# Norm sums behind the first product, gate transposes in the pool mixer, the last down third by tokens, and operands placed with their weights

## The chip, the cores and the metric

One core of one Trainium2 chip runs the whole program. The metric is the device time of one execution in microseconds (us). TensorE (PE) multiplies; PEld is its weight load, which overlaps; VectorE (DVE), ScalarE (ACT) and GpSimd (POOL) work elementwise; SyncE (SP) only issues DMAs, and so does ACT for some.

## The reference

Two transformer blocks in fp32 on x of 512 tokens by 1024 features, one after the other:

```
first_block:  u = rms_norm(x, norm_in_g);  pool_x, pool_z, m_x, m_z = split(u @ w_in)
              y_pool = pool_mixer(pool_x) * silu(pool_z)
              y_m    = mlstm(m_x: conv, headwise q/k/v, gates, both directions) * silu(m_z)
              h = rms_norm(x + [y_pool, y_m] @ w_out, norm_out_g)
second_block: h += nsa_mixer(rms_norm(h, norm_mix[0]))          # three attention branches
              h += conv_ffn(rms_norm(h, norm_ffn[0]))           # layer 0
              h += swa_mixer(rms_norm(h, norm_mix[1]))          # window 128, sinks
              h += conv_ffn(rms_norm(h, norm_ffn[1]))           # layer 1
              return rms_norm(h, norm_final)
conv_ffn(h):  a, u = split(h @ w_gu);  (silu(causal_conv3(a)) * u) @ w_down     # 2816 wide
rms_norm(x,g) = x * rsqrt(mean(x*x) + 1e-6) * g
```

## The kernel before

Activations lie feature-major: `H` is [128 partitions, 8 chunks of features, 512 tokens]. Every operand of a product is split into a rounded high part (`xh`, `wh`: a cast on ACT) and a rest (`xl`, `wl`: a subtraction on DVE). `linear` makes one 128x512 output from 8 chunks (6 or 8 in the down product) by three matmuls each, `mm3`: wh·xh (L108), wh·xl (L109), wl·xh (L110), so 24 matmuls of 128 rows by 512 columns. The activation moves, the weight is stationary. A unit of weights (`raw`, L93: 512 KB by an SP DMA into `wr`; `wh`, L102; `wl`, L103) feeds one linear; `wr`, `wh` and `wl` have 3 buffers each.

An rms norm is not applied before the product. `norm_x` splits H times its gain, the products run on that, and each result is multiplied by the row `rb` of 1/rms per token when it leaves PSUM. `rb` comes from `norm_r`: eight squares on ACT (`accsq`, L182), seven additions (L187, six on POOL and the last on DVE, 3 buffers `sq`), a column sum on PE (`colsum`, L152), a Newton iteration on DVE (L140 to L146), a broadcast on PE (`bcast`, L159) and a copy on ACT (L162). At each of the five norms two linears are issued ahead of `norm_r`, and their results wait in PSUM (six banks for linears: two `mm`, three `S`, one `po`).

Stages in order: `first_block` (the 8 m_x linears with a conv, `gates`, the pool mixer, mLSTM, w_out), `nsa`, `ffn(0)`, `swa`, `ffn(1)`, the final norm. `gates` makes a chain of scans on DVE of 36 rows (`gi`, `gB`, `gM`) and transposes gi and gB by eight small matmuls (L294, L295); the columns are used in mLSTM.

The feed-forward takes its 22 hidden chunks in segments of 8, 8 and 6: up(0), up(1), down(0), up(2), down(1), then the last third. Before, `down_last` runs it for tokens 0 to 255, then for 256 to 511: 16 linears of 18 matmuls of 256 columns, each with its own unit of 768 columns, loaded and split twice. `final_half` (squares L1192, additions L1194, column sum L1199, Newton, broadcast L1205, copy L1208, scaling L1214 to L1217, DMA L1218) follows for each half of the tokens, the first one in the middle of the second half's linears.

The order on each engine is a scheduler's: it takes the instructions in code order with their dependences and moves them by readiness, so one product's matmuls may stand inside another's. Where a tile lies in a partition of SBUF follows from the order in which the pools `con`, `per`, `wp` and those of the stages hand out tiles, summed up in bytes: before, `xh`, `xl`, `wh` and `wl` begin at multiples of 128 bytes, the `gh` and `gl` of the feed-forward 64 bytes past one, the pool mixer's `yph` and `ypl` 96 past one, and mLSTM's `mqh`, `mql`, `mkh`, `mkl` 32 past one.

Of the kernel before, what the change touches and what calls it, by code (L numbers as in the profile page):

```python
# [11 lines left out]
F32 = mybir.dt.float32  # L12
# [19 lines left out]

class Model:
    def __init__(self, ctx, tc, a, out, stop=None):
# [18 lines left out]
    def first_loads(self):  # L53
        nc, a = self.nc, self.a
        vec = self.con.tile([128, a["vecs"].shape[1]], F32, name="vec")
        nc.scalar.dma_start(vec, a["vecs"])
        nc.sync.dma_start(self.H[:, 0:1, :], a["xT"][:, 0:1, :])
        self.first = self.unit(a["w_in"], 0)
        for k0, k1 in ((1, 2), (2, 4), (4, 6), (6, 8)):
            nc.sync.dma_start(self.H[:, k0:k1, :], a["xT"][:, k0:k1, :])  # L60
        self.vec, self.voff = vec, VOFF

# [85 lines left out]

    def colsum(self, acc):
# [45 lines left out]
    def norm_r(self):  # L195

        acc = None
        for k in range(KC):
            acc = self.accsq(k, acc)
        y = self.rstd(acc)  # L200
# [63 lines left out]
    def gates(self, lp, pp, gps):  # L264
        nc = self.nc
        V, G, S, PE = nc.vector, nc.gpsimd, nc.scalar, nc.tensor
        t = lambda s: pp.tile([36, T], F32, name=s)
        g, lf, ex, B, M = t("gi"), t("lf"), t("gex"), t("gB"), t("gM")
# [21 lines left out]
        V.tensor_copy(identr, self.ident[:36, :36])  # L290
        tp = self.tp_ps([128, 2, NT, 36])
# [8 lines left out]
        self.gate_tiles = (gcol, ecol, nmh, nml, identr)  # L300

    def pool_mixer(self, pp, xh, xl, rb):
        nc, a = self.nc, self.a
        V, G, S, PE = nc.vector, nc.gpsimd, nc.scalar, nc.tensor
        W = T + 16
        pinv = pp.tile([128, 4, 16], F32, name="pinv")
# [4 lines left out]
        for g, w in enumerate(POOL_WINDOWS):  # L311
# [3 lines left out]
            for i in range(2):  # L315
# [20 lines left out]
                pl.append(l)  # L336
            if g % 2 == 0:
                pw = self.unit(a["pool_w"], g // 2)
# [183 lines left out]
    def mid_norm_r(self):  # L522
# [13 lines left out]
        rb = self.per.tile([128, T], F32, name=self.n("rb"), tag="rb", bufs=1)  # L536
        self.bcast(y2, rb)
        return rb, y1

    def rot_half(self, pool, src):  # L540

        r = self.per.tile([128, T], F32, name=self.n("rot"), tag="sq", bufs=3)
# [4 lines left out]
    def rope(self, pool, ps, cs, out, bias=None):  # L547
        V, G, S = self.nc.vector, self.nc.gpsimd, self.nc.scalar
        x = self.per.tile([128, T], F32, name=self.n("sq"), tag="sq", bufs=3)
# [85 lines left out]
    def nsa(self):  # L635
        tc, nc, a = self.tc, self.nc, self.a
        V, G, S, PE = nc.vector, nc.gpsimd, nc.scalar, nc.tensor
        with tc.tile_pool(name="nsa", bufs=1) as ap:
            self.attn_consts(ap)
# [19 lines left out]
            pre = [self.linear(a["nsa_w"], i, xh, xl, wide=True) for i in range(2)]  # L659
            rb, y1 = self.mid_norm_r()  # L660
# [75 lines left out]
            def cproj(kv, pre=None):  # L736
                blk = [ap.tile([128, 8, 124], F32, name=self.n("blk"), tag="p", bufs=4) for _ in range(2)]
                for m in range(2):
                    ps = pre[m] if pre else self.linear(a["nsa_w"], 2 * kv + m, xh, xl, wide=True)
# [27 lines left out]
            bk = cproj(0, pre)  # L767
# [75 lines left out]
    def cmp_vals(self, ap, p, pc, vbd):  # L843
# [6 lines left out]
        pct = self.per.tile([64, T], F32, name=self.n("pct"), tag="sq", bufs=3)  # L850
# [117 lines left out]
    def swa_tables(self):  # L968
        tc, nc, a = self.tc, self.nc, self.a
        V, G = nc.vector, nc.gpsimd  # L970
        ap = self.swa_early = self.ctx.enter_context(tc.tile_pool(name="swae", bufs=1))
# [14 lines left out]
    def swa(self):  # L986
# [4 lines left out]
        with tc.tile_pool(name="swa", bufs=1) as ap:  # L991
            cs = (cos, sin)
            xh, xl = self.norm_x("norm_mix1")
            pre = [self.linear(a["swa_w"], i, xh, xl, wide=True) for i in range(2)]
            rb = self.norm_r()
            Q, O = {}, {}

            def proj(i, wide=False):
                ps = pre[i] if i < 2 else self.linear(a["swa_w"], i, xh, xl, wide=wide)
# [120 lines left out]
            wo(1, range(8), True)  # L1120


    def ffn(self, l):
        tc, nc, a = self.tc, self.nc, self.a
        V, G, S, PE = nc.vector, nc.gpsimd, nc.scalar, nc.tensor
        if l:
            self.fin = self.ctx.enter_context(tc.tile_pool(name="fin", bufs=1))
        with tc.tile_pool(name=f"ffn{l}", bufs=1) as fp:
            xh, xl = self.norm_x(f"norm_ffn{l}")
            pre = [self.linear(a[f"ffn_gu{l}"], i, xh, xl, wide=True) for i in range(2)]  # L1130
            rb = self.norm_r()
            cw, cb = f"ffn_cw{l}", f"ffn_cb{l}"

            def up(seg):
                f0, nf = SEGS[seg]
                gh, gl = [], []
                for f in range(f0, f0 + nf):
                    ps = pre[0] if f == 0 else self.linear(a[f"ffn_gu{l}"], 2 * f, xh, xl, wide=True)
# [9 lines left out]
                    ps = pre[1] if f == 0 else self.linear(a[f"ffn_gu{l}"], 2 * f + 1, xh, xl, wide=True)  # L1148
# [12 lines left out]
            def down_last(g):  # L1161

                nf = SEGS[2][1]
                for hf in range(2):
                    c = slice(256 * hf, 256 * hf + 256)
                    gh, gl = [[x[:, c] for x in g[i]] for i in range(2)]
                    for m in range(KC):
                        ps = self.linear(a[f"ffn_d{l}2"], m, gh, gl, nk=nf, wide=True, n=256)
                        V.tensor_tensor(self.H[:, m, c], ps[:, :256], self.H[:, m, c], op=OP.add)
                        if hf and m == 3:  # L1170
                            self.final_half(0)
# [5 lines left out]
            down(1, g1)  # L1177
            if l:
                down_last(g2)
            else:  # L1180
                down(2, g2)

    def final_half(self, hf):

        nc, fp = self.nc, self.fin
        V, G, S, PE = nc.vector, nc.gpsimd, nc.scalar, nc.tensor
        W, nb = 256, 2
        c = slice(W * hf, W * hf + W)
        acc = None
        for k in range(KC):  # L1190
            d = fp.tile([128, W], F32, name=self.n("fs"), tag="fs", bufs=3)
            S.activation(d, self.H[:, k, c], AF.Square)  # L1192
            if k:
                V.tensor_tensor(acc, acc, d, op=OP.add)  # L1194
            else:
                acc = d
        ps = self.tp_ps([128, nb])
        for j in range(nb):
            PE.matmul(ps[:, j:j + 1], acc[:, j * 128:(j + 1) * 128], self.ones, start=True, stop=True)  # L1199
        var = self.con.tile([128, nb], F32, name=self.n("fv"), tag="fv", bufs=2)  # L1200
        V.tensor_scalar(var, ps, 1.0 / D, EPS, op0=OP.mult, op1=OP.add)
        y = self.newton(var, nb)
        pb = self.tp_ps([128, W])
        for j in range(nb):
            PE.matmul(pb[:, j * 128:(j + 1) * 128], y[:, j:j + 1].to_broadcast([128, 128]), self.ident,  # L1205
                      start=True, stop=True)
        rb = fp.tile([128, W], F32, name=self.n("frb"), tag="frb", bufs=2)
        S.copy(rb, pb)  # L1208
        ov = self.out.rearrange("(k p) t -> p k t", p=128)
        for k2 in range(KC // 2):  # L1210
            for k in (2 * k2, 2 * k2 + 1):
# [161 lines left out]
```

## Time and profile before

| | |
|---|---|
| median of 3 runs | 1666.68 us (1666.2 to 1668.69) |
| the profiled execution | 1669.42 us, of which the span from first to last instruction is 1667.7 |
| PE busy | 1611.2 us, 97% |
| weight loads (PEld) | 1309.0 us, 78%, beside the matmuls |
| DVE, ACT, POOL busy | 1085.1 us, 796.5 us, 251.7 us (65%, 48%, 15%) |
| granted TensorE clock | 0.990 of full over the span |
| data moved | 145.41 MB, mean 87 GB/s |

All times below are from the profiled execution, counted from its first instruction. A row of the timeline gives start, duration, engine, line, operation, the tile written and the tiles read, and in brackets how long the engine had been idle and what released it. A matmul's duration includes its way through the array, so the pace of a stretch is read from the starts.

### The profile page before, as it was taken

The page shows a single profiled execution, that of the slowest core. Times are in us where ns is not written, and L with a number is a line of the kernel's source. Part 1 is how long each engine was busy: PE and PEld are TensorE (multiplying, and loading weights), DVE is VectorE, ACT ScalarE, POOL GpSimd, SP SyncE. Part 2 cuts the span into 40 slices and gives each one's busy share as a digit, 9 for nine tenths or more (in the row PEclk, how much of TensorE's full clock was granted, in tenths as well). Part 3 has the DMA queues.
Part 4 walks back from the last instruction along what each step waited for, and adds up shares of the span by engine and source line. Part 5 has one row for each costly group of instructions (what it writes and reads, how often), then busy time and mean ns, then how long its engine had stood idle before and what let it go on. Part 6 is the DMA issues. An engine that isn't in the chain of part 4 may idle for free. (4 is left out here: it accounts for less than half of the span.)

```text
span 1667.7 us, 21687 instructions
## 1 busy us (share of the span) xinstructions
PE 1611.2 (97%) x7988; PEld 1309.0 (78%) x7988; DVE 1085.1 (65%) x1888; ACT 796.5 (48%) x1525; POOL 251.7 (15%) x310
## 2 busy tenths in 40 slices
PE   7999999999799999999999999998999999999996
PEld 5678788878677777778888888887787888888886
DVE  5776557866779999986555345356988555535447
ACT  4532255554248877764333233145876433323323
POOL 3000000132212122122111001023312111100001
PEclk9999999999999999999999999999999999999998
DMA  4223311123341121103332322233321232322323
GB/s 155 96 77 98 101 65 53 51 84 102 101 131 43 37 62 39 49 24 120 100 101 90 101 90 100 83 107 92 109 77 56 96 101 91 99 98 92 101 89 127
DMA packets 47113, 145.41 MB, mean 87 GB/s; under 512 B 6752, under 2 KB 9056, under 8 KB 47008
## 3 DMA queue, kind: packets, MB, share of 16 engines
q1 hardware_dynamic: 45424, 141.65, 26.6%
q10 hardware_dynamic: 1584, 2.39, 0.5%
q8 instruction: 63, 1.03, 0.2%
q14 instruction: 42, 0.34, 0.1%
HBM read 133.13 MB, written 2.10 MB: 81 GB/s over the span
## 5 line engine op out<-in xcount | busy, mean ns | idle before, releaser
L102 ACT CAST wh<-wr 128x1024 fp32r<-128x1024 f32 (+2 forms) x241 | 247.2, 1026 | 494.5 <-PE S L109 208.0
L103 DVE TENSOR_TENSOR wl<-wr,wh 128x1024 fp32r<-128x1024 f32 (+2 forms) x232 | 282.5, 1219 | 40.4 <-ACT wh L102 39.6
L108 PE MATMUL mm<-xh,wh 128*128 128x512 f32 (+1 forms) x584 | 233.8, 400 | 0.4 <-ACT xh L130 0.4
L109 PE MATMUL mm<-xl,wh 128*128 128x512 f32 (+1 forms) x584 | 232.2, 398 | 2.0 <-DVE xl L134 2.0
L110 PE MATMUL mm<-xh,wl 128*128 128x512 f32 (+1 forms) x584 | 231.8, 397 | 0.0
L108 PE MATMUL S<-xh,wh 128*128 128x512 f32 x512 | 200.4, 391 | 8.3 <-ACT wh L102 8.3
L109 PE MATMUL S<-xl,wh 128*128 128x512 f32 x512 | 200.4, 391 | 0.1
L110 PE MATMUL S<-xh,wl 128*128 128x512 f32 x512 | 200.0, 391 | 0.0
L109 PEld LDWEIGHTS mm<-xl,wh 128*128 128x128 f32 (+1 forms) x584 | 110.3, 189 | 25.6 <-DVE xl L134 3.2
L108 PEld LDWEIGHTS mm<-xh,wh 128*128 128x128 f32 (+1 forms) x584 | 110.4, 189 | 22.6 <-issue 1.0
L110 PEld LDWEIGHTS mm<-xh,wl 128*128 128x128 f32 (+1 forms) x584 | 110.1, 189 | 21.5
L108 PEld LDWEIGHTS S<-xh,wh 128*128 128x128 f32 x512 | 96.6, 189 | 28.4 <-ACT wh L102 8.3
L110 PEld LDWEIGHTS S<-xh,wl 128*128 128x128 f32 x512 | 96.5, 188 | 20.7 <-DVE wl L103 0.8
L109 PEld LDWEIGHTS S<-xl,wh 128*128 128x128 f32 x512 | 96.5, 188 | 20.6 <-DVE xl L134 0.7
L187 POOL TENSOR_TENSOR sq<-sq,sq 128x512 f32<-128x512 f32 x36 | 60.2, 1673 | 159.9 <-ACT sq L182 151.6
L131 DVE TENSOR_TENSOR ptl<-tp,pth 128x512 fp32r<-128x512 f32 (+1 forms) x112 | 73.6, 663 | 6.8 <-ACT pth L130 6.0
L889 ACT ACTIVATE p<-S,nm 128x128 f32<-128x128 f32 (+3 forms) x128 | 67.1, 532 | 10.6 <-DVE nm L885 5.3
L130 ACT CAST pth<-tp 128x512 fp32r<-128x512 f32 (+1 forms) x112 | 62.9, 573 | 18.8 <-PE tp L612 16.0
L1140 POOL MEMSET fa<- 128x2 f32 x44 | 4.2, 98 | 446.8 <-DVE fc L1145 446.8
L108 PE MATMUL S<-gh,wh 128*128 128x512 f32 (+1 forms) x194 | 71.5, 369 | 0.0
L109 PE MATMUL S<-gl,wh 128*128 128x512 f32 (+1 forms) x194 | 71.5, 369 | 0.0
L110 PE MATMUL S<-gh,wl 128*128 128x512 f32 (+1 forms) x194 | 71.5, 369 | 0.0
(435 smaller groups left out, 3545.8 us busy)
## 6 DMA issues: line engine op xcount, KB each, us to landing
wr<-ffn_gu SPq DMA_DIRECT2D x88, 512.0 KB, 3.5
wr<-w_in SPq DMA_DIRECT2D x32, 512.0 KB, 3.3
wr<-ffn_d SPq DMA_DIRECT2D x32, 512.0 KB, 3.4
wr<-nsa_w SPq DMA_DIRECT2D x20, 512.0 KB, 3.5
wr<-ffn_d SPq DMA_DIRECT2D x24, 384.0 KB, 3.0
wr<-w_out SPq DMA_DIRECT2D x16, 512.0 KB, 3.5
rot<-sq SPq DMA_DIRECT2D x92, 64.0 KB, 2.0
wr<-swa_w SPq DMA_DIRECT2D x10, 512.0 KB, 3.4
```

Of the source, the lines that this page charges most:

```text
L102: nc.scalar.copy(h[:, :cols], r[:, :cols])
L103: (nc.gpsimd if self.wpool else nc.vector).tensor_tensor(l[:, :cols], r[:, :cols], h[:, :cols], op=OP.subtract)
L108: mm(ps, wh, xh, start=first, stop=False)
L109: mm(ps, wh, xl, start=False, stop=False)
L110: mm(ps, wl, xh, start=False, stop=last)
L130: nc.scalar.copy(h, src)
L131: nc.vector.tensor_tensor(l, src, h, op=OP.subtract)
L187: e.tensor_tensor(acc, acc, dst, op=OP.add)
L889: S.activation(t[:, :w], sb[b], AF.Exp, bias=nm[:, 0, h, b:b + 1], accum_out=nm[:, 1, h, b:b + 1])
L1140: G.memset(t[:, 0:2], 0.0)
```

## The change

- `first_loads`: an activation on a 1-element tile loads ACT's table at once; the first unit is cast and subtracted in pieces of 256 and 768 columns.
- `norm_first`: the norm's sums are issued behind the first linear, and one or two more linears behind them (three in all at the four later norms). `accsq` has 5 buffers; the last two additions stand on DVE (`late=2`), at the first norm all seven.
- `gate_cols` with the eight transposes is called in the pool mixer, ahead of its second group's products.
- `place` puts a pad of 8 or 16 floats at the head of a stage's pool; `warm` and a `vec` shorter by 8 columns move all that follows. Afterwards `wh`, `wl`, `xh`, `xl`, `gh`, `gl`, `yph`, `ypl` begin 64 bytes past a multiple of 128. Counting 512-column matmuls by how far the moving tile's start lies from that of the weights loaded next, modulo 128: 4143 at the same place and 1432 elsewhere before, 5532 and some 190 after.
- The last third of layer 1 is done by blocks of 128 tokens with the weights moving: four transposes bring H into the bank, 18 matmuls of 512 columns add the product, twice for each block, so the result has tokens on partitions. Its six units are loaded and split inside down(1). The final norm is a sum along the row (`accum_out` of a Square), one Newton column, two scalings and two DMAs for each block; `out` is token-major.

```diff
+PADS = {"l0a": 8, "nsa": 16, "swa": 0, "ffn0": 16, "ffn1": 0}
 def first_loads(self):
+        warm = self.con.tile([128, 1], F32, name="warm")
+        nc.gpsimd.memset(warm, 0.0)
+        nc.sync.dma_start(self.H[:, 0:1, :], a["xT"][:, 0:1, :])
         nc.scalar.dma_start(vec, a["vecs"])
-        nc.sync.dma_start(self.H[:, 0:1, :], a["xT"][:, 0:1, :])
-        self.first = self.unit(a["w_in"], 0)
+        nc.scalar.activation(warm, warm, AF.Copy, scale=1.0)
...
+        nc.sync.dma_start(r, a["w_in"][0])
+        for c in (slice(0, 256), slice(256, 1024)):
+            nc.scalar.copy(h[:, c], r[:, c])
+            nc.vector.tensor_tensor(l[:, c], r[:, c], h[:, c], op=OP.subtract)
...
-    def accsq(self, k, acc, scale=None):
+    def accsq(self, k, acc, scale=None, late=2):
-        dst = self.per.tile([128, T], F32, name=self.n("sq"), tag="sq", bufs=3)
+        dst = self.per.tile([128, T], F32, name=self.n("sq"), tag="sq", bufs=5)
-            e = nc.vector if k == KC - 1 else nc.gpsimd
+            e = nc.vector if k >= KC - late else nc.gpsimd
+    def norm_first(self, lin, norm_y, n=3):
+        pre = [lin(0)]
+        y = norm_y()
+        pre += [lin(i) for i in range(1, n)]
+        return pre, y
 def first_block
-            pre = [self.linear(a["w_in"], m, xh, xl, wide=True, pre=self.first if m == 0 else None)
-                   for m in range(2)]
-            rb = self.norm_r()
+            pre, y = self.norm_first(
+                lambda m: self.linear(a["w_in"], m, xh, xl, wide=True, pre=self.first if m == 0 else None),
+                lambda: self.norm_y(KC), 2)
+            rb = self.norm_row(y)
 def pool_mixer
+            if g == 1:
+                self.gate_cols()
 def nsa (and alike in swa and ffn)
-            pre = [self.linear(a["nsa_w"], i, xh, xl, wide=True) for i in range(2)]
-            rb, y1 = self.mid_norm_r()
+            pre, (y2, y1) = self.norm_first(lambda i: self.linear(a["nsa_w"], i, xh, xl, wide=True),
+                                            self.mid_norm_y)
+            rb = self.norm_row(y2)
 def ffn
-            def down(seg, g):
+            def down(seg, g, more=None, ws=None):
+                    if more and 1 <= m < 7:
+                        ws.append(next(more))
+            def down_last(g, ws):
+                for j in range(NT):
+                    tc_ = slice(128 * j, 128 * j + 128)
...
+                    for hf in range(2):
+                        c = slice(512 * hf, 512 * hf + 512)
+                        ps = self.wide_ps()
+                        for i in range(4):
+                            mm(ps[:, 128 * i:128 * i + 128], self.H[:, 4 * hf + i, tc_], self.ident,
+                               start=i == 0, stop=False, is_transpose=True)
+                        for f in range(nf):
+                            gh, gl = g[0][f][:, tc_], g[1][f][:, tc_]
+                            wh, wl = ws[f][0][hf], ws[f][1][hf]
+                            mm(ps, gh, wh, start=False, stop=False)
+                            mm(ps, gl, wh, start=False, stop=False)
+                            mm(ps, gh, wl, start=False, stop=f == nf - 1)
+                        S.activation(sq, ps, AF.Square, scale=1.0 / 32, accum_out=ss[:, hf:hf + 1])
+                        if hf == 0:
+                            V.tensor_tensor(o[:, c], ps, self.nf[:, c], op=OP.mult)
+                    V.scalar_tensor_tensor(ss[:, 2:3], ss[:, 0:1], EPS, ss[:, 1:2], op0=OP.add, op1=OP.add)
+                    y = self.newton_col(ss[:, 2:3])
+                    S.mul(o[:, 0:512], o[:, 0:512], y)
+                    nc.scalar.dma_start(self.out[tc_, 0:512], o[:, 0:512])
+                    V.scalar_tensor_tensor(o[:, 512:], ps, y, self.nf[:, 512:], op0=OP.mult, op1=OP.mult)
+                    nc.sync.dma_start(self.out[tc_, 512:], o[:, 512:])
```

How the rows stand on the engines, at the places in question (the number behind a name tells apart the tiles of one name). On PE at the start of the program, before: the column sum (tp, from sq) behind two whole linears, `S_135` (not shown) and `S_166`, and ahead of the third, `mm_268`.

```order
L108 MATMUL S_166<-xh_131,wh_162 128x512
L109 MATMUL S_166<-xl_132,wh_162 128x512
L110 MATMUL S_166<-xh_131,wl_163 128x512
L152 MATMUL tp_214<-ones,sq_191 128x1 x4
L108 MATMUL mm_268<-xh_103,wh_264 128x512
```

The same place on PE after, from the end of the first linear (`S_140`); `S_217` is the second and `mm_273` the third.

```order
L128 MATMUL S_140<-xh_136,wl_76 128x512
L126 MATMUL S_217<-xh_108,wh_213 128x512
L127 MATMUL S_217<-xl_109,wh_213 128x512
L126 MATMUL mm_273<-xh_108,wh_269 128x512
L127 MATMUL mm_273<-xl_109,wh_269 128x512
L128 MATMUL S_217<-xh_108,wl_214 128x512
L126 MATMUL S_217<-xh_112,wh_213 128x512
L127 MATMUL S_217<-xl_113,wh_213 128x512
L183 MATMUL tp_188<-ones,sq_165 128x1 x4
L128 MATMUL S_217<-xh_112,wl_214 128x512
```

The column sum moved from behind the second linear to within it, and two matmuls of the third linear stand ahead of it.

On ACT at the start, after, from the last split of H on: the casts of the second and third weights (`wh_213`, `wh_269`).

```order
L151 ACTIVATE xh_136<-H,vec 128x512
L213 ACTIVATE sq_176<-H 128x512
L213 ACTIVATE sq_179<-H 128x512
L213 ACTIVATE sq_182<-H 128x512
L213 ACTIVATE sq_185<-H 128x512
L120 CAST wh_213<-wr_211 128x1024
L120 CAST wh_269<-wr_267 128x1024
```

All eight squares stand ahead of those casts; before, the second weight's cast came behind the third square.

On PE at the gates, before: the first transpose of gi (tp from gi) stands inside the linear `S_622`, the first of the pool mixer.

```order
L110 MATMUL S_622<-xh_115,wl_619 128x512
L108 MATMUL S_622<-xh_119,wh_618 128x512
L294 MATMUL tp_554<-ident,gi 128x36
L109 MATMUL S_622<-xl_120,wh_618 128x512
L110 MATMUL S_622<-xh_119,wl_619 128x512
```

After, all eight stand together behind the linear `S_802`, five linears (about 120 rows of PE) later than before.

```order
L127 MATMUL S_802<-xl_137,wh_798 128x512
L128 MATMUL S_802<-xh_136,wl_799 128x512
L343 MATMUL tp_842<-ident,gi 128x36
L344 MATMUL tp_842<-ident,gB 128x36
```

The linear `S_622`'s matmuls no longer have a transpose between them.

## Rows read from the trace of the kernel before

**Rows 1.** The page: busy time by engine; one group (count, busy us, mean ns)

```profile
PE 1611.2 (97%) x7988; PEld 1309.0 (78%) x7988; DVE 1085.1 (65%) x1888; ACT 796.5 (48%) x1525; POOL 251.7 (15%) x310
...
L103 DVE TENSOR_TENSOR wl<-wr,wh 128x1024 fp32r<-128x1024 f32 (+2 forms) x232 | 282.5, 1219 | 40.4 <-ACT wh L102 39.6
```

**Rows 2.** PE's waits over the span: who waited for whom, total, times, longest

```profile
PE S L1020 <- DVE qs L576: 5.0, 1, 5.0
...
PE mm L109 <- DVE xl L134: 2.0, 3, 0.8
```

**Rows 3.** Timeline of PE, first 37 us

```profile
25.62 1.56 PE L152 MATMUL tp<-ones,sq 128*128 128x1 f32 x8 [3.64 <-DVE sq L187]
...
36.22 0.39 PE L108 MATMUL S<-xh,wh 128*128 128x512 f32 x1
```

**Rows 4.** Stretch of PE behind that wait: busy (instructions), granted clock, DMA share, GB/s

```profile
27.05:32.70 5.65, 5.65 (x14) 0.50 0.29 93
```

**Rows 5.** Timeline of ACT, first 12 us

```profile
5.32 1.28 ACT L133 ACT_TABLE_LOAD   x1 [5.32 <-DMA H<-xT]
6.62 0.72 ACT L133 ACTIVATE xh<-H,vec 128x512 fp32r<-128x512 f32 x1
7.25 1.03 ACT L102 CAST wh<-wr 128x1024 fp32r<-128x1024 f32 x1
...
8.80 0.62 ACT L182 ACTIVATE sq<-H 128x512 f32<-128x512 f32 x1
9.33 1.32 ACT L133 ACTIVATE xh<-H,vec 128x512 fp32r<-128x512 f32 x2
```

**Rows 6.** Timeline of POOL, first 36 us

```profile
13.60 11.24 POOL L187 TENSOR_TENSOR sq<-sq,sq 128x512 f32<-128x512 f32 x5
```

**Rows 7.** Timeline of PE at the gates

```profile
88.47 0.22 PE L294 MATMUL tp<-ident,gi 36*128 36x36 f32 x1 [2.75 <-DVE gi L281]
...
91.58 0.25 PE L295 MATMUL tp<-ident,gB 36*128 36x36 f32 x1 [0.60 <-DVE gB L284]
```

**Rows 8.** Timeline of PE, up(2) of layer 1: first and last of 22 matmuls

```profile
1535.75 0.39 PE L108 MATMUL mm<-xh,wh 128*128 128x512 f32 x1
...
1540.51 0.39 PE L108 MATMUL S<-xh,wh 128*128 128x512 f32 x1
```

**Rows 9.** Timeline of PE, down(1) of layer 1: first and last of 19

```profile
1594.87 0.39 PE L108 MATMUL po<-gh,wh 128*128 128x512 f32 x1
...
1599.07 0.39 PE L108 MATMUL po<-gh,wh 128*128 128x512 f32 x1
```

**Rows 10.** Timeline of PE, w_out on the pool mixer's output: first and last of 28

```profile
214.50 0.40 PE L108 MATMUL S<-yph,wh 128*128 128x512 f32 x1
...
220.80 0.40 PE L108 MATMUL S<-yph,wh 128*128 128x512 f32 x1
```

**Rows 11.** Timeline of PE, mLSTM: first and last of 13

```profile
262.56 0.39 PE L108 MATMUL S<-mqh,mkh 128*128 128x512 f32 x1
...
265.28 0.39 PE L108 MATMUL S<-mqh,mkh 128*128 128x512 f32 x1
```

**Rows 12.** Timeline of PE, the last third and the end

```profile
1617.27 0.28 PE L108 MATMUL mm<-gh,wh 128*128 128x256 f32 x1
...
1651.25 0.28 PE L110 MATMUL mm<-gh,wl 128*128 128x256 f32 x1
1655.08 0.99 PE L1199 MATMUL tp<-ones,fs 128*128 128x1 f32 x4 [3.56 <-DVE fs L1194]
1658.58 1.19 PE L1205 MATMUL tp<-ident,nwy 128*128 128x128 f32 x4 [2.52 <-DVE nwy L146]
```

**Rows 13.** Timeline of DVE, the end

```profile
1660.22 3.56 DVE L1217 SCALAR_TENSOR_TENSOR H<-H,vec,frb 128x256 f32<-128x256 f32 x5 [1.78 <-ACT frb L1208]
```

**Rows 14.** Timeline of PE in the attention: eight transposes in one go

```profile
506.83 1.04 PE L612 MATMUL tp<-ident,p 128*128 128x128 f32 x8
```

**Rows 15.** Groups of ACT's instructions by shape over the span

```profile
L889 ACT ACTIVATE p<-S,nm 128x512 f32<-128x512 f32 x32 | 22.0, 691 | 1.5 <-DVE nm L885 1.3
```

More of the change, by code (lines that the diff above doesn't have):

```diff
@@ L61, in first_loads, with place @@
         self.vec, self.voff = vec, VOFF
+    def place(self, pool, name):
+        if PADS[name]:
+            pool.tile([128, PADS[name]], F32, name="pad" + name)
     def v(self, name, i=0, n=1):
@@ L147, in newton, with newton_col @@
         return y
+    def newton_col(self, var):
+        V = self.nc.vector
+        t = lambda s, d=F32: self.con.tile([128, 1], d, name=self.n(s), tag="c" + s, bufs=2)
+        yi, y, hv, q = t("nwi", I32), t("nwy"), t("nwh"), t("nwq")
+        V.tensor_single_scalar(yi, var.bitcast(I32), 1, op=OP.logical_shift_right)
+        V.tensor_scalar(y.bitcast(I32), yi, -1, 0x5F3759DF, op0=OP.mult, op1=OP.add)
+        V.tensor_scalar(hv, var, -0.5, None, op0=OP.mult)
+        for it in range(3):
+            V.scalar_tensor_tensor(q, y, hv, y, op0=OP.mult, op1=OP.mult)
+            V.scalar_tensor_tensor(y, q, 1.5, y, op0=OP.add, op1=OP.mult)
+        return y
     def colsum(self, acc):
@@ L305, in pool_mixer @@
         W = T + 16
+        self.place(pp, "l0a")
         pinv = pp.tile([128, 4, 16], F32, name="pinv")
@@ L548, in rope @@
         V, G, S = self.nc.vector, self.nc.gpsimd, self.nc.scalar
-        x = self.per.tile([128, T], F32, name=self.n("sq"), tag="sq", bufs=3)
+        x = self.per.tile([128, T], F32, name=self.n("sq"), tag="sq", bufs=5)
         if bias is None:
@@ L638, in nsa @@
         with tc.tile_pool(name="nsa", bufs=1) as ap:
+            self.place(ap, "nsa")
             self.attn_consts(ap)
@@ L849, in cmp_vals @@
             PE.transpose(ct[:, j * 128:(j + 1) * 128], pc[:, j].rearrange("p h c -> p (h c)"), self.ident)
-        pct = self.per.tile([64, T], F32, name=self.n("pct"), tag="sq", bufs=3)
+        pct = self.per.tile([64, T], F32, name=self.n("pct"), tag="sq", bufs=5)
         S.copy(pct, ct)
@@ L1127, in ffn @@
             self.fin = self.ctx.enter_context(tc.tile_pool(name="fin", bufs=1))
+            self.nf = self.fin.tile([128, D], F32, name="nf")
+            nc.scalar.dma_start(self.nf, bass.AP(tensor=a["norm_final"].tensor, offset=a["norm_final"].offset,
+                                                 ap=[[0, 128], [1, D]]))
         with tc.tile_pool(name=f"ffn{l}", bufs=1) as fp:
+            self.place(fp, f"ffn{l}")
             xh, xl = self.norm_x(f"norm_ffn{l}")
-            pre = [self.linear(a[f"ffn_gu{l}"], i, xh, xl, wide=True) for i in range(2)]
-            rb = self.norm_r()
+            pre, y = self.norm_first(lambda i: self.linear(a[f"ffn_gu{l}"], i, xh, xl, wide=True), self.norm_y)
+            rb = self.norm_row(y)
+            gu = lambda i: pre[i] if i < 3 else self.linear(a[f"ffn_gu{l}"], i, xh, xl, wide=True)
             cw, cb = f"ffn_cw{l}", f"ffn_cb{l}"
@@ L1176, in ffn @@
             g2 = up(2)
-            down(1, g1)
+            ws = []
+            down(1, g1, last_weights() if l else None, ws)
             if l:
-                down_last(g2)
+                down_last(g2, ws)
             else:
                 down(2, g2)
[L1183 to L1211, printed above, removed]
-                h, g = self.H[:, k, c], self.v("norm_final", k)
-                if k % 3 == 1:
-                    S.mul(h, h, g)
-                    G.tensor_tensor(h, h, rb, op=OP.mult)
-                else:
-                    V.scalar_tensor_tensor(h, h, g, rb, op0=OP.mult, op1=OP.mult)
-            nc.sync.dma_start(ov[:, 2 * k2:2 * k2 + 2, c], self.H[:, 2 * k2:2 * k2 + 2, c])
@@ L1371 @@
     r = run_bass_kernel_spmd(nc, [A], core_ids=[0])
-    return np.ascontiguousarray(r.results[0]["out"].T)[None]
+    return np.ascontiguousarray(r.results[0]["out"])[None]
```

110 lines of the change are left out of this document (63 added, 47 removed).

## The prediction

> **What bounds the kernel now.** I read the page first, then PE's waits, then the timeline of PE and of the engine that it waits for at each longer wait, then the starts of matmuls in long stretches. PE is busy 97% of the span [rows 1], so the bound is PE, and there are two ways to gain: the idle stretches of PE, and its pace while busy. Idle stretches that the change can reach are the start [rows 3], the two waits at the gates [rows 7], the wait of 5.0 us in the window attention and 2.0 us at the last feed-forward's norm [rows 2], and the end [rows 12]. The pace is not one number. In up(2) 21 steps take 4.76 us, 226.7 ns each [rows 8]; in down(1) 18 steps take 4.20 us, 233.3 ns [rows 9]; with the pool mixer's output as the moving tile 27 steps take 6.30 us, 233.3 ns [rows 10]. Same shape, same 24-matmul linears: 6.6 ns apart, or 2.9%. What differs is where the moving tile begins: at the weights' place modulo 128 bytes in the fast stretch, 64 and 96 bytes off in the slow ones.
>
> **Start, -5.5 us.** Before, ACT cannot begin the first split before its table is loaded (1.28 us, at 5.32, once H's first piece is there) [rows 5]. Two linears follow; then PE idles 3.64 us ahead of the column sum at 25.62, since POOL makes five additions in 11.24 us, 2.2 us each [rows 3, 6]. [...] The fourth linear begins at 36.22 [rows 3].
> After, the table load lies in the wait for H. ACT's queue then holds eight splits, eight squares, the first weights and the second's cast in that order. At the distances of [rows 5] (split 0.63, from 6.62 to 7.25; square 0.53, from 8.80 to 9.33; cast about 0.95) that is 5.4 + 8 x 0.63 + 8 x 0.53 + 0.95 + 1.0 = 16.6 us. The last split leaves ACT at some 13.5, so the first linear ends at about 15.2, and PE waits some 1.5 us for the second weights, which now stand behind the squares: a new wait, left of the old one's 3.64. The third weights come 0.95 later, at 17.6, and from there PE has all it needs: the additions are on DVE and the sum is ready near 18.5, while the column sum stands four matmuls further on. [...]
>
> **Gates, -3.5 us.** PE waits 2.75 us for gi and 0.60 for gB in the middle of a linear [rows 7]. The eight transposes move behind four more linears, over 20 us later, when the scans have long ended. Both waits go, and 0.2 us of refilling behind them. What they gave to is late only in mLSTM, 100 us on. One more table load on ACT (1.28) is hidden: ACT is busy 48% [rows 1]. Ends 3.0 and 3.9.
>
> **Operand places, -7.5 us.** Slow matmuls that become equal: the three down products of layer 0 and two of layer 1, (8 + 8 + 6) x 24 + (8 + 8) x 24 = 912, and 8 x 24 = 192 on the pool mixer's output, 1104 by 6.6 ns = 7.3 us; some 140 scattered ones more would make 8.2. I take 7.5. The new place of almost everything, both tiles at 64, does not occur before; what bounds it is mLSTM, where both begin at 32: 12 steps in 2.72 us, 226.7 ns [rows 11]. So equality seems to count, not the multiple of 128. Ends: 0 and -8.2, and on the other side the rival below.
> [...]
>
> **Later norms, +0.5 us.** With the sum behind the first linear, PE reaches it when the squares are just done; the row rb comes up to 1.8 us later than now because the broadcast stands behind a whole third linear. Six banks hold the results, and a third linear is there to cover 5.4 us. The 5.0 us in the window attention hang on DVE's rotated queries [rows 2]: rb later by 1.8, one linear more in front; bounds -1.4 and +1.5, I take 0. At the last feed-forward the wait for xl stays, and two additions of 128x512 on DVE come behind it, about 0.7 each (an estimate from the 691 ns of the nearest row of that shape [rows 15]): 0 to +1. The 512 KB of the final gain go on ACT's queue there, one issue. Sum +0.5.
>
> **Last third, -6.5 us.** Before, it begins at 1617.27 and the last matmul at 1651.25; then PE idles 3.56 and 2.52 us around the column sum and the broadcast, DVE scales from 1660.22 for 3.56 us to 1663.8, and the last DMA ends with the span at 1667.7, 3.9 us later [rows 12, 13].
> After: 8 groups of four transposes and 18 matmuls of 512 columns. Eight transposes take 0.80 us from the first to the next instruction's start [rows 14], so four take 0.40; 18 x 0.227 = 4.08; together 4.48 x 8 = 35.8, and PE is done at 1653.1, 1.6 us later than before. Behind it: 0.2 to leave the array, the Square from PSUM 0.69 by ACT's exponential of the same shape [rows 15], one addition and nine steps of Newton. Thirteen such steps take at most 2.5 us in before (between 1656.07, the column sum's end, and 1658.58 [rows 12]), 0.19 each, so 1.9. Then one scaling of 128x512, about 0.75, and the DMA of the same size as before's, 3.9. 1653.1 + 0.2 + 0.7 + 1.9 + 0.75 + 0.1 of handing over + 3.9 = 1660.7 to 1661.5 with waits between engines: 6.2 to 7.0 gained. The other three blocks' ends lie under the next blocks' 9 us of matmuls.
> What it adds lies in down(1): six units more, one for each linear of 5.4 us, each 512 KB and a cast and a subtraction of 1024 columns (1.03 on ACT [rows 5], 1.22 on DVE [rows 1]). DVE's work per linear is then two subtractions and one addition to H of about 0.7, some 3.1 of 5.4 us. The sixteen units of 768 columns in the last third go, so nothing is to be fed there. If none of it were hidden, six units would cost 6 x (1.03 + 1.22) = 13.5 us.
>
> **Sum.** -5.5 - 3.5 - 7.5 + 0.5 - 6.5 = -22.5. The profiled execution took 1669.42, so 1646.9; it lies 2.7 above the median of the runs, which gives 1644.2 for the median.
>
> **Rivals.**
> 1. Places don't matter, and down is slow for another reason, such as its unit of weights or what runs beside it. For it: the slow stretches are few kinds of product. Against: w_out and down have the same 233.3 and share nothing but the offset [rows 9, 10]. Then 7.5 stay: 1651.7. [...]
> 2. The moving tile must begin at a multiple of 128, or of 32 without 64, to be fast, and equal places at 64 are slow. Then the whole of the kernel but attention goes at 233.3: the 4143 that are fast now lose 6.6 ns each, 27.3 us, and the gain of 7.5 is not had. 1644.2 + 34.8 = 1679, slower by 12. It decides from about 3400 slow matmuls on. For it: no row has both at 64. Against: both at 32 is fast [rows 11].
> 3. down(1) starves: nothing of the six units is hidden, 13.5 us, and the last third begins that much later: 1657.7. For it: two units per linear through three buffers. Against: at 87 GB/s on average the DMAs are far from what the start moves, and DVE and ACT have room [rows 1].
> 4. PE pays for the sums' new place: the start gives 3 of its 5.5, and the four later norms each cost 1 us more: 2.5 + 4 = 6.5, so 1650.7. For it: PE cannot pass a column sum that waits. Against: of these norms' products only the last one's shows a wait now [rows 2].
>
> **Chances.** My forecast 0.74, rival 1 0.09, rival 2 0.07, rival 3 0.04, rival 4 0.06. No change means within 0.2%, 3.3 us, about what a measurement of this kernel can tell. Slower is rival 2, 0.07; of the other 0.93 I give 0.03 to no change, for several of them together; faster 0.90. The ends of the terms (start 2.5, gates 0.5, later norms 2.5, last third 2 and the little that places may give more) added as squares are some 5 us each way, and the range goes on up to rivals 1 and 4 and part of 3: 1637 to 1655.
>
> **What would show it.** Start: the fourth linear's first matmul near 30; a table load before 5 us; a PE wait for a wh cast after the first linear; if starts lie 0.43 us apart near 20 us the clock fell. Gates: no PE wait for gi or gB. Places: starts 226.7 ns apart in down, in w_out and (rival 2) in up; a pace of 233 in up(2) would make the forecast wrong by itself. Last third: eight groups of about 4.5 us, and some 8 us from the last matmul to the end. Wrong it is, too, if PE waits inside down(1), or if PE's wait in the window attention grows by more than 2 us.

## The result and the profile after

The changed kernel takes 1655.8 us, median of 4 runs (1654.98 to 1656.44), against 1666.44 (1665.68 to 1668.69) for the kernel before on the same chip: ratio 0.9932, 95% interval 0.9919 to 0.9945. It is faster by 10.6 us, not by the 22.5 forecast; the time lies 0.8 above the range's upper end. A second measurement of the same program gave 0.9931 (e5).

The profiled execution of after took 1655.41 us (span 1653.7), close to its median. That of before took 1669.42, which is 3.0 above the median of its runs here, so the two profiles are 14.0 us apart and the runs 10.6. The stages below are differences of the profiles, taken from the start of the same piece of work in each.

| stage | forecast | measured |
|---|---|---|
| start | -5.5 | -6.4 |
| gates and the pool mixer's first product | -3.5 | +1.8 |
| operand places | -7.5 | -4.8 |
| later norms | +0.5 | about -1.4 |
| window attention | 0 (inside the later norms) | +2.9 |
| last third and end | -6.5 | -6.0 |

The first part of the page, busy time of each engine [rows 1 is before's]:

```profile
PE 1604.0 (97%) x7860; PEld 1302.9 (79%) x7860; DVE 1076.7 (65%) x1878; ACT 790.6 (48%) x1520; POOL 226.3 (14%) x294
```

PE is still the bound, busy 7.2 us less. PE's waits over the span (who waited for whom, total, times, longest):

```profile
PE S L1075 <- DVE qs L626: 5.9, 1, 5.9
...
PE po L666 <- DVE ot L679: 5.0, 5, 1.7
...
PE mm L126 <- POOL up L369: 3.9, 1, 3.9
...
PE tp L183 <- DVE sq L218: 1.3, 2, 0.7
...
PE mm L127 <- DVE xl L152: 0.5, 1, 0.5
```

Against [rows 2, 7] the waits for gi and gB are gone, but one of 3.95 us stands at the pool mixer's first product, and in the window attention the wait for the rotated queries is 5.9 instead of 5.0 and the accumulator's (`ot`) 5.0 us in all, which was 1.7 before.

The start, timeline of PE (start, length, work, and in brackets the idle time before it and its releaser):

```profile
16.02 0.50 PE L126 MATMUL S<-xh,wh 128*128 128x512 f32 x1 [0.70 <-ACT wh L120]
...
18.70 0.95 PE L183 MATMUL tp<-ones,sq 128*128 128x1 f32 x8
...
29.82 0.39 PE L126 MATMUL S<-xh,wh 128*128 128x512 f32 x1
```

The column sum waits no longer [rows 3], the new wait for the second weights is 0.70 (two more of 0.2 follow it), and the fourth linear begins at 29.82 instead of 36.22.

The gates, timeline of PE, then of DVE, then of POOL:

```profile
91.35 0.47 PE L126 MATMUL mm<-pqh,wh 128*128 128x512 f32 x1 [3.95 <-POOL up L369]
```

```profile
77.05 0.68 DVE L316 SCALAR_TENSOR_TENSOR lf<-lf,gex 36x512 f32<-36x512 f32 x1 [11.17 <-ACT gex L315]
...
85.43 0.68 DVE L330 SCALAR_TENSOR_TENSOR nml<-gM,nmh 36x512 fp32r<-36x512 f32 x1
86.15 0.69 DVE L370 TENSOR_TENSOR up<-mm,rb 128x512 f32<-128x512 f32 x1
...
89.90 1.29 DVE L383 SCALAR_TENSOR_TENSOR sw<-sw,up 128x512 f32<-128x512 f32 x2
```

```profile
86.22 0.11 POOL L368 MEMSET up<- 128x8 f32 x1 [82.05 <-DVE nml L330]
```

PE names POOL, whose memset had ended 5 us earlier. What PE waits for is `pq`, at the end of a chain on DVE: eight steps of the gates with one subtraction of weights among them (77.05 to 86.1), then `up`, the window sums and `sw`. POOL's memset of `up` was released by the gates' last row `nml` (last line above): the mixer's pool takes the space that the gates' pool leaves. From the gates' sums to the first product the chain takes 20.9 us; before it took 21.4. It was as long before, but PE spent part of it in the two waits at the transposes, and the transposes and products filled more of it.

The same stretch by windows (busy and instructions of PE, granted clock, DMA share, GB/s), of after and of before:

```profile
86.00:92.00 6.00, 2.05 (x10) 1.00 0.20 59
92.00:98.00 6.00, 6.00 (x21) 0.72 0.35 124
```

```profile
92.00:98.00 6.00, 6.00 (x30) 1.00 0.11 25
```

Behind the new wait the clock falls to 0.72 of full over 6 us: from 92.78 to 95.77 us the matmuls start 0.43 us apart and not 0.227, as before's do from 28.04 to 32.31 us, where the clock is 0.50 [rows 4].

The window attention: its first matmul on PE, the first use of the row `rb` on DVE, the longest DVE step on the way to the rotated queries `qs`, and PE's first product with them; before, then after:

```profile
1113.24 0.39 PE L108 MATMUL po<-xh,wh 128*128 128x512 f32 x1
1130.42 0.69 DVE L1001 TENSOR_TENSOR pj<-po,rb 128x512 f32<-128x512 f32 x1 [1.93 <-ACT rb L162]
1139.89 4.11 DVE L558 TENSOR_TENSOR kf<-kf,rot 128x512 f32<-128x512 f32 x1 [1.12 <-POOL rot L556]
1149.88 0.58 PE L1020 MATMUL S<-kd,qs 128*128 128x256 f32 x1 [5.04 <-DVE qs L576]
```

```profile
1104.10 0.39 PE L126 MATMUL po<-xh,wh 128*128 128x512 f32 x1
1123.09 0.69 DVE L1056 TENSOR_TENSOR pj<-po,rb 128x512 f32<-128x512 f32 x1 [4.82 <-ACT rb L193]
1130.02 6.86 DVE L607 TENSOR_TENSOR qf<-sq,cos 128x512 f32<-128x512 f32 x1 [0.84 <-ACT sq L603]
1142.54 0.58 PE L1075 MATMUL S<-kd,qs 128*128 128x256 f32 x1 [5.93 <-DVE qs L626]
```

Counted from the stage's first matmul, `rb` is used at 19.0 us instead of 17.2, and PE's product with the queries comes at 38.4 instead of 36.6. From the first use of `rb` to that product it is 19.45 us in both, so by the traces these 1.8 us come from `rb`. The other 1.1 of the stage's 2.9 lie behind that product.

Places: layer 0's down, then layer 1's up(2) and down(1), first and last matmul of each:

```profile
924.81 0.39 PE L127 MATMUL mm<-gl,wh 128*128 128x512 f32 x1
...
929.79 0.39 PE L128 MATMUL mm<-gh,wl 128*128 128x512 f32 x1
...
1527.09 0.39 PE L126 MATMUL S<-xh,wh 128*128 128x512 f32 x1
...
1531.85 0.39 PE L126 MATMUL S<-xh,wh 128*128 128x512 f32 x1
...
1575.68 0.40 PE L126 MATMUL S<-gh,wh 128*128 128x512 f32 x1
...
1579.88 0.40 PE L126 MATMUL S<-gh,wh 128*128 128x512 f32 x1
```

22 steps in 4.98 us are 226 ns each in layer 0, as forecast; 21 steps in 4.76 us are 226.7 in up(2), with both tiles at 64; 18 steps in 4.20 us are 233.3 in layer 1's down, as slow as before [rows 9].

The last third and the end, timeline of PE, then of DVE:

```profile
1609.29 0.60 PE L1250 MATMUL S<-ident,H 128*128 128x128 f32 x4
...
1646.07 0.40 PE L1257 MATMUL po<-lw,gh 128*128 128x512 f32 x1
```

```profile
1647.22 0.16 DVE L1262 SCALAR_TENSOR_TENSOR ss<-ss 128x1 f32<-128x1 f32 x1 [3.94 <-ACT fs L1259]
...
1649.21 0.75 DVE L1266 SCALAR_TENSOR_TENSOR fo<-po,nwy,nf 128x512 f32<-128x512 f32 x1
```

Eight groups take 36.8 us (4.6 each), and 7.6 us lie between the last matmul's start and the span's end; before, it was 16.4 [rows 12].

### The profile page after: what moved, and what is told of

It is laid out like the page before. It is cut to its first block, busy times and chain, and to the rows that moved or that the text cites. A ratio compares the mean times of both kernels' runs of the same rounds, so it can differ in the third digit from the quotient of the medians.

```text
span 1653.7 us, 21346 instructions
## 1 busy us (share of the span) xinstructions
PE 1604.0 (97%) x7860; PEld 1302.9 (79%) x7860; DVE 1076.7 (65%) x1878; ACT 790.6 (48%) x1520; POOL 226.3 (14%) x294
## 4 chain that ended last, share of the span: by engine, by line
PE 81%; DVE 11%; ACT 4%; issue 3%; POOL 0%; DMA 0%; DVEq 0%; POOLq 0%; ACTq 0%
PE S L126 10%; PE S L128 10%; PE S L127 10%; PE mm L126 9%; PE mm L127 9%; PE mm L128 9%; PE po L126 3%; PE po L127 3%; PE po L128 3%; PE tp L662 2%; PE po L666 1%; PE po L667 1%; DVE wl L121 1%; DVE blk L981 1%; DVE ptl L149 1%
## 5 line engine op out<-in xcount | busy, mean ns | idle before, releaser
L120 ACT CAST wh<-wr 128x1024 fp32r<-128x1024 f32 (+1 forms) x224 | 233.1, 1043 | 486.4 <-PE S L127 208.4
L121 DVE TENSOR_TENSOR wl<-wr,wh 128x1024 fp32r<-128x1024 f32 (+1 forms) x215 | 264.6, 1231 | 51.2 <-ACT wh L120 35.9
L126 PE MATMUL mm<-xh,wh 128*128 128x512 f32 (+1 forms) x568 | 226.4, 399 | 0.7 <-ACT xh L148 0.4
L127 PE MATMUL mm<-xl,wh 128*128 128x512 f32 (+1 forms) x568 | 225.2, 396 | 0.5 <-DVE xl L152 0.5
L128 PE MATMUL mm<-xh,wl 128*128 128x512 f32 (+1 forms) x568 | 224.8, 396 | 0.0
L127 PEld LDWEIGHTS mm<-xl,wh 128*128 128x128 f32 (+1 forms) x568 | 106.6, 188 | 22.1 <-DVE xl L152 1.2
L126 PE MATMUL po<-xh,wh 128*128 128x512 f32 x184 | 71.8, 390 | 0.0
L127 PE MATMUL po<-xl,wh 128*128 128x512 f32 x184 | 71.7, 390 | 0.0
L128 PE MATMUL po<-xh,wl 128*128 128x512 f32 x184 | 71.6, 389 | 0.0
L1207 ACT ACTIVATE fc<-fc 128x512 f32<-128x512 f32 x44 | 27.9, 634 | 78.8 <-DVE fc L1206 78.8
```

Source lines behind the costliest of these rows:

```text
L120: nc.scalar.copy(h[:, :cols], r[:, :cols])
L121: (nc.gpsimd if self.wpool else nc.vector).tensor_tensor(l[:, :cols], r[:, :cols], h[:, :cols], op=OP.subtract)
L126: mm(ps, wh, xh, start=first, stop=False)
L127: mm(ps, wh, xl, start=False, stop=False)
L128: mm(ps, wl, xh, start=False, stop=last)
L1207: S.activation(c, c, AF.Silu)
```

## The experiments

Each was timed in five rounds against the kernel before on the same chip. Unless it says so, the edit is to the changed kernel; its own ratio to compare with is 0.9931 [0.9918, 0.9945]. The intervals of e1, e2, e6 and e7 overlap with that one, so what they show rests on the stretch of the profile that the edit touches.

**e1: layer 1's gate tiles moved by 384 bytes, to the weights' place.**

```diff
-PADS = {"l0a": 8, "nsa": 16, "swa": 0, "ffn0": 16, "ffn1": 0}
+PADS = {"l0a": 8, "nsa": 16, "swa": 0, "ffn0": 16, "ffn1": 96}
```

> Changed kernel with the pad of layer 1's feed-forward at 96 floats instead of 0, so that gh and gl begin at the weights' place modulo 512 bytes (now equal modulo 128 only, 128 off modulo 256). Theory 1, the place counts over more than 128 bytes: starts in down(0), down(1) and the last third 226.7 ns apart instead of 233.3; 528 matmuls x 6.6 ns = 3.5 us faster than the changed kernel's 1655.8, so 1652.3. Theory 2, those stretches are slow for a reason that isn't the place: 233.3 ns as before, 1655.8, within 1.

1652.49 us, 0.9905 [0.989, 0.9919]. Down(1), first and last of 23 matmuls:

```profile
1574.72 0.39 PE L126 MATMUL S<-gh,wh 128*128 128x512 f32 x1
...
1579.70 0.39 PE L127 MATMUL S<-gl,wh 128*128 128x512 f32 x1
```

22 steps in 4.98 us: 226.4 ns. Layer 1's stretch is 3.1 us shorter: 2.5 in the two downs, 0.5 in the last third. With the change's own pad, gates and weights are 128 bytes apart (448 and 320 modulo 512) and slow; now they are equal and fast.

**e2: the gates' transposes back at the gates.**

```diff
         self.gate_tiles = (nmh, nml, identr)
+        self.gate_cols()
...
-            if g == 1:
-                self.gate_cols()
```

> Changed kernel with the eight gate transposes called at the end of gates again, as in the kernel before. Theory 1, a chain from the gate sums over ACT, the scans on DVE and the pool mixer's first two tiles to its first product (20.9 us after the change, 21.4 before) sets the time there and the transposes' waits lie in its shadow: waits of some 3 us return at the transposes, the 3.9 us in front of the first product go, total 1654 to 1656. Theory 2, as predicted, the waits at the transposes are time of their own: 3.5 us slower than 1655.8, so 1659.

1653.74 us, 0.9914 [0.9899, 0.9929]. Timeline of PE:

```profile
82.25 0.22 PE L344 MATMUL tp<-ident,gi 36*128 36x36 f32 x1 [2.79 <-DVE gi L323]
...
85.42 0.25 PE L345 MATMUL tp<-ident,gB 36*128 36x36 f32 x1 [0.68 <-DVE gB L326]
```

Both waits are back, the one at the mixer is gone, and the stage ends 1.6 us earlier than in after. The old waits cost nothing: they lay beside the same chain.

**e3: the first group's two z linears ahead of its products.**

```diff
-            for i in range(2):
-                m = 2 * g + i
+            def gate(i):
...
+                return z
+            zs = [gate(i) for i in range(2)] if g == 0 else None
+            for i in range(2):
+                m = 2 * g + i
+                z = zs[i] if zs else gate(i)
```

> Changed kernel with both z linears of the pool mixer's first group ahead of its two products (the second was between them). [...] Theory 2, DVE stays behind for the whole group and PE waits at the second group instead: 1655 to 1657.

1649.99 us, 0.9896 [0.9879, 0.9912]: the 1650 to 1652 that one linear more of work in front of the wait (5.4 us, 24 x 226.7 ns) and a whole clock behind it were to give. Timeline of PE, then the clock by windows:

```profile
89.83 0.50 PE L128 MATMUL mm<-xh,wl 128*128 128x512 f32 x1 [2.00 <-DVE wl L121]
```

```profile
92.00:98.00 6.00, 6.00 (x28) 1.00 0.34 121
```

The stage is 3.5 us shorter; the rest of this run's lead lies in the two attentions (1.6 and 0.9 by the profiles), which the edit doesn't touch. A second linear covers the chain, though its weights' subtraction stands behind the same DVE work, so that 2.00 of the wait remain.

**e4: the weights' subtractions in the window attention on DVE.**

```diff
-            self.wpool = True
+            self.wpool = False
```

> Changed kernel with the weights' subtractions in the window attention on DVE instead of POOL. Theory 1, the three waits of 1.5 to 1.65 us there (one in the kernel before) come from a DVE scaling held up beside POOL's 2.6 us subtraction: no scaling over 1 us, the waits go, 2 to 4 us faster, 1652 to 1654. Theory 2, DVE is what PE waits for in this stage and 16 subtractions of 1.2 us more make it later: 1658 to 1665.

1647.23 us, 0.9873 [0.9858, 0.9888]; the stage itself, from its first product to the next feed-forward's, is 8.0 us shorter than in after (the whole profile 7.4, as the pool mixer, untouched, lost 0.9 to the clock). Timeline of after, first DVE, then POOL, then e4's waits of PE:

```profile
1202.46 0.35 DVE L1092 TENSOR_SCALAR p<-p,nm 128x256 f32<-128x256 f32 x1
...
1204.80 2.47 DVE L1092 TENSOR_SCALAR p<-p,nm 128x256 f32<-128x256 f32 x1
```

```profile
1204.53 2.59 POOL L121 TENSOR_TENSOR wl<-wr,wh 128x1024 fp32r<-128x1024 f32 x1 [4.26 <-ACT wh L120]
```

```profile
PE S L1075 <- DVE qs L626: 3.0, 1, 3.0
...
PE po L666 <- DVE ot L679: 1.4, 2, 1.1
```

The same scaling takes 0.35 us alone and 2.47 when POOL has begun its subtraction. In after six DVE operations of the attention are held so: five take 1.83 to 2.66 us, and `qf` (0.69 elsewhere) takes 6.86 while POOL makes a subtraction and three products of its own in one go. In before two are (4.11 and 2.51). In e4 the longest of the 32 scalings takes 1.33, the median 0.35 (after: 2.47 and 0.35). PE idles for no weights in this stage, so what e4 gains is the price of the hold-ups; whether they make the 2.9 us that the change added here is another question (e10). By what means POOL holds DVE up is not shown by any run.

**e5: the changed kernel again.**

> The changed kernel again, to have it on the same chip as the three that follow: 0.9932 of the kernel before, within the interval of that ratio (0.9919 to 0.9945).

1655.68 us, 0.9931 [0.9918, 0.9945]. The wait at the mixer (4.0), the clock of 0.72 in 92 to 98 us and the waits in the window attention (5.9 for the queries, 4.5 for `ot`) all came again, so none of them is an accident of the one profile. The size of the clock's fall is one, though: e1 and e4 have the same work and the same wait of 3.9 there, and over the 6 us behind it the clock is 0.52 and 0.55; they lose 1 us more by it.

**e6: without the pads of the pool mixer and of layer 0's feed-forward.**

```diff
-PADS = {"l0a": 8, "nsa": 16, "swa": 0, "ffn0": 16, "ffn1": 0}
+PADS = {"l0a": 0, "nsa": 16, "swa": 0, "ffn0": 0, "ffn1": 0}
```

> Changed kernel with the pads of the pool mixer and of layer 0's feed-forward at 0, so yph lies 32 bytes and layer 0's gh 64 bytes off the weights' place modulo 256. Theory 1, the place modulo 256 sets the pace: 192 and 528 matmuls (and some 48 of the pool product) go from 226.7 to 233.3 ns, 4.8 to 5.1 us slower than the changed kernel. Theory 2, a place counts only together with something else of those stages: less than 2 us slower.

1659.0 us, 0.9949 [0.9937, 0.9962]. By stage +1.3 at w_out and +3.5 in layer 0's down, what 192 and 528 matmuls at 6.6 ns make (1.3 and 3.5).

**e7: the sums behind the last linear but one.**

```diff
-        pre = [lin(0)]
+        pre = [lin(i) for i in range(n - 1)]
         y = norm_y()
-        pre += [lin(i) for i in range(1, n)]
+        pre += [lin(i) for i in range(n - 1, n)]
```

> Changed kernel with the sums of the four later norms behind the second linear again (the first norm as changed, two late additions on DVE kept). Theory 1: at layer 0's feed-forward PE no longer waits for the sum (0.7 and 0.5 us there now), the other three don't move: 1 to 2 us faster than the changed kernel. Theory 2, the sums' place is worth what layer 1's feed-forward gained at its norm (1.7 us): 1 to 2 us slower. No difference over 0.5 us at the sliding-window norm by either.

1653.45 us, 0.9917 [0.9904, 0.993]; 2.4 us by the profiles, of which 1.0 at layer 0's feed-forward norm and 0.8 at layer 1's; the second was not expected by either theory. In after, PE waits at layer 0's:

```profile
745.73 0.50 PE L127 MATMUL mm<-xl,wh 128*128 128x512 f32 x1 [0.46 <-DVE xl L152]
...
748.52 1.05 PE L183 MATMUL tp<-ones,sq 128*128 128x1 f32 x8 [0.67 <-DVE sq L218]
```

**e8: e1, e3 and e4 together.**

> Changed kernel with the pad of 96 in layer 1's feed-forward, both z linears of the first pool group ahead of its products, and the window attention's subtractions on DVE. If the three gains lie in different stages they add up: 3.1 + 5 to 6 + 7.4 by the stages of their profiles, 16 us faster than the changed kernel. If one of them only moves a wait that a later stage gives back, 10 or less.

1642.71 us, 0.985 [0.9837, 0.9864]: 13.0 under e5, where the three alone make 17.3 (3.2, 5.7 and 8.4 against e5) and 16 were expected. By the profiles the largest part that is missing lies at the pool mixer, 1.9 gained there instead of 3.5; the window attention gives 7.2 instead of 8.0. At the mixer the wait of 2.00 is the same, the clock isn't:

```profile
92.00:98.00 6.00, 6.00 (x24) 0.85 0.41 135
```

**e9: before, with the places made equal** (in the mixer's pool and the feed-forwards').

```diff
+                pp.tile([128, 8], F32, name="padl0a")
...
+            fp.tile([128, 16], F32, name=f"padffn{l}")
```

> The kernel before with nothing but two pads, 8 floats ahead of the pool mixer's tiles and 16 ahead of both feed-forwards', so that yph, gh and their rests begin at the weights' place modulo 256 bytes. Theory 1, the place modulo 256 sets the pace: 912 and 192 matmuls go from 233.3 to 226.7 ns, 7.3 us faster than the kernel before (the term as predicted). Theory 2, the pace is bound to something else of the change: within 1 us of the kernel before.

1660.2 us, 0.9955 [0.9942, 0.9967]: 7.4 us by the runs. In the profile the 1104 matmuls of 512 columns are 7.4 shorter too, so the forecast's term was right for before; it is the changed layout of layer 1 that did not get its share. That the two numbers are equal is luck: the profile is 10.3 shorter in all, of which 2.4 in the window attention and 0.8 at the start, which the pads don't touch, while the last third, whose matmuls have 256 columns, became slower. Its first and last matmul:

```profile
1605.91 0.28 PE L108 MATMUL mm<-gh,wh 128*128 128x256 f32 x1
...
1641.49 0.28 PE L110 MATMUL mm<-gh,wl 128*128 128x256 f32 x1
```

From start to start these are 35.58 us, and 33.98 in before [rows 12], there at a clock of 1.00; over the whole program the clock is 0.989 in e9 and 0.987 to 0.991 in before. Most steps there are 113 to 114 ns in before, 64 bytes apart; the 1.60 us more with equal places are 5.6 ns for each of the 287 steps: for this shape the place that is fast for 512 columns is the slow one.

**e10: before, with the window attention's subtractions on DVE.** The edit is that of e4.

> The kernel before with the window attention's subtractions on DVE instead of POOL. Theory 1, the hold-ups beside POOL's subtraction are the kernel's and not the change's, and only their number is chance (one long one before, three after): 3 to 6 us faster than the kernel before, with the wait for the rotated queries (5.0) shorter by 2 to 3. Theory 2, the change brought them: less than 2 us faster.

1661.95 us, 0.9961 [0.9948, 0.9973]. The window attention is 7.6 us shorter in the profile (170.2 to 162.6), nearly the 8.0 of e4 (173.1 to 165.1), and the wait for the rotated queries falls from 5.0 to 1.4. So what e4 gains was to be had in before too, and with the hold-ups gone from both kernels the changed one is still 2.5 us longer here: POOL's subtractions can be put down for 0.4 of the 2.9 us that the change added. At the gates, which the edit doesn't touch, the profile lost 2.3: the wait for gi is the same 2.8, but the clock behind it isn't (before: 1.00, above), and PE is so late that it doesn't wait for gB:

```profile
92.00:98.00 6.00, 6.00 (x23) 0.79 0.26 91
```

**e11: e8 with e7.**

> The run of the three edits together (1642.7) with the later norms' sums behind the second linear as well: another 1.5 to 2.4 us if that gain adds, 1640 to 1641; 1642 to 1643 if the stages behind give it back.

1640.38 us, 0.9831 [0.9817, 0.9844]: the fastest, 27.2 us under the kernel before. Its profile is 2.8 us under e8's: 1.8 come from the two feed-forward norms and 1.6 from the mixer, where the clock stays whole (1.00 in 92 to 98 us) behind the same wait of 2.00; other stages give 0.6 back.

**e12: e11, with the first group's z weights subtracted on POOL.**

```diff
+            self.wpool = g == 0
             zs = [gate(i) for i in range(2)] if g == 0 else None
+            self.wpool = False
```

> The kernel of the run before this one, with the subtraction of the second z weight of the pool mixer's first group on POOL. Theory 1, PE's wait of 2.0 us there and the fall of its clock behind it come from that subtraction's place in DVE's queue behind the scans: the wait goes to 1 us or less and the clock stays, 2 to 3 us faster than that kernel. Theory 2, the cast that precedes it on ACT is as late itself, or POOL's 2.4 us take as long: within 1 us.

1642.28 us, 0.9848 [0.9834, 0.9861]: no gain over e11, so the theory that this removes the last wait falls; it is 1.9 slower, which the other theory (within 1 us) didn't expect either. PE's waits for such weights, the longest of each kind being there:

```profile
PE mm L128 <- POOL wl L121: 1.7, 1, 1.7
...
PE mm L126 <- ACT wh L120: 1.4, 2, 1.2
```

The subtraction is slower on POOL (2.35 us, and 1.22 on DVE in after) and takes DVE's place as the late one; the clock there was 0.80 in 92 to 98 us.

## Why the prediction was wrong, point by point

- **Start: right**, 0.9 better. The short wait for the second weights came (0.70, forecast 1.5), and the clock stayed at 1.00 behind it (16 to 30 us). The 5.5 were a choice between a whole clock behind that wait and one that falls as in [rows 4]; no run shows that value, and what the trace shows is 6.4 with the clock whole behind a wait of 0.70.
- **Gates: wrong, +1.8 instead of -3.5.** The step that failed is "Both waits go, and 0.2 us of refilling behind them". The waits go, and with each of them 0.11 us of a longer first step (in before 0.34 instead of 0.227, 88.62 to 88.96 and 92.13 to 92.47); but the prediction did not ask what PE reaches next. The chain through DVE's scans to the first product was as long as before, and PE had work for only 16.9 of its 20.9 us. e2 shows that the old waits cost nothing, e3 that another linear in front gains 3.5. About 1.7 of the loss is the clock behind the wait: the twelve steps from 91.35 to 95.77 take 4.42 us, which at 226.7 ns would be 2.7.
- **Places: mis-sized, -4.8 instead of -7.5.** The step "at the weights' place modulo 128 bytes in the fast stretch" had the wrong modulus: what the runs show for matmuls of 512 columns is modulo 256. 0 and 256 bytes apart run at 226.7 ns (layer 0's feed-forward is 256 apart); modulo 256 distances of 128 (after's down(1)), 192 and 224 [rows 9, 10] run at 233.3. Of the 5532 matmuls counted as equal in the change, 384 in layer 1's down and most of the last third's 144 are 128 apart. So layer 1's down gained nothing (2.5 us; e1 gains them, and 0.5 in the last third), and layer 0 and w_out gained 3.5 and 1.3. Rival 1 is excluded by e6 and e9, rival 2 by up(2) of the changed kernel itself, which runs at 226.7 with both tiles at 64. The last third's products, with the weights moving, run at 233 too, nearly 1 us over the forecast's 0.227; the 0.5 that e1's pad gains there are 3.5 ns for each of the 144.
- **Later norms: within the bounds as a sum, by luck**, about -1.4. Layer 0's feed-forward lost 1.7, as rival 4 said of each, layer 1's gained 1.7 where 0 to +1 was forecast, and the first attention's stage gained 1.4, but it is 1.6 shorter still in e3 and e6, whose edits don't touch it. e7 shows that at the two feed-forwards the sums are better one linear later.
- **Window attention: wrong, +2.9 instead of 0.** The step that failed is "rb later by 1.8, one linear more in front; bounds -1.4 and +1.5, I take 0". `rb` did come 1.8 later, and the linear in front covered none of it: PE's product with the queries came 1.8 later. e7 puts the sum back and `rb` comes as late, so it is the broadcast behind a third whole linear; no run takes that linear away. The cause of the other 1.1 is open: this part of the stage is 2.4 shorter in e9, whose pads don't touch it. The hold-ups beside POOL, which the prediction did not look for, cost 8 us in the changed kernel and 7.6 in before (e4, e10), so they are a gain to be had in both, and by these two runs 0.4 of the 2.9.
- **Last third: right**, -6.0. Down(1) takes 44.6 us as before, the added units of weights starved nothing, so rival 3 is excluded. The 0.2 us that the forecast gave the last matmul to leave the array are 0.20 in the trace: it starts at 1646.07, a step is 0.23, and the Square starts at 1646.50.
- **Median.** Gates, places and window attention make 5.3 + 2.7 + 2.9 = 10.9 us too little; start and norms give 2.8 back and the last third 0.5 less than forecast: 8.6, and the profiles differ from the forecast by 8.5. The other 3.1 are in the runs: the forecast put the median 2.7 below the profiled execution, and after's median lies 0.4 above it. Why is open; that before's clock at the gates was whole, unlike e10's, does not explain it.

## What to carry to other kernels

When a wait is moved away, follow the chain behind it to the next instruction that the bound engine waits for: if the chain is as long and less work covers it, the wait comes back later, with what the clock loses behind it (here 3.95 us, and 1.7 by the clock). A rule read from a few rows (equal places modulo 128) must be tried against the numbers that the new layout really has, above all where it has a distance that no row shows. When a row of results comes later, look how much later its last reader on the bound engine comes, and not only whether other work stands in front. And work given to another engine is not free where that engine holds up the one that it relieves (here 8.0 us, e4).

## What the hardware did that was not expected

- TensorE's pace hangs on the distance between the moving tile's and the weights' places. With 512 columns it is 226.7 ns at 0 or 256 bytes and 233.3 at 128, 192 and 224 modulo 256, 7.4 us of the kernel before (e9). With 256 columns it is the other way round: 113 to 114 ns at 64 bytes (before), and 5.6 more at equal places (e9, 35.58 us for 287 steps instead of 33.98).
- The clock behind a wait of 2 to 4 us differs between executions and programs at the same place. Over the 6 us behind the wait it was 0.72 (after, e5), 0.52 (e1) and 0.55 (e4) behind 3.9 us; 1.00 (e3, e11) and 0.72 (e8) behind 2.00; 1.00 (before, e2, e9) and 0.64 (e10, in 86 to 92 us) behind 2.75 to 2.8. By the matmuls' starts it is worth 1.7 us in after and e8, 2.6 in e4 and 2.8 in e1, and its cause stays open.
- In after a DVE scaling of 128x256 beside a POOL subtraction took seven times as long as the median one, 2.47 us for 0.35, and a product of 128x512 beside four POOL operations in one go ten times, 6.86 for 0.69. Both executions of the changed kernel (after, e5) have the wait of 5.9 us for the queries that lies behind the latter.
